# The first layer's recurrence gates as products of high and low parts, in a two-layer hybrid mixer on one core

## The chip, the core and the metric

The kernel runs on one core of a Trainium2 chip. The metric is the device time of one execution in microseconds (us), as a median over runs. TensorE (PE in the rows) multiplies, VectorE (DVE) and ScalarE (ACT) do elementwise work, GpSimd (POOL) fills tiles, and SyncE (SP) issues most of the transfers from memory.

## The reference

Two layers work on 256 context tokens and 256 latent tokens, 1024 wide, in float32. Each layer has a token mixer with three parallel branches behind one input projection (a long convolution, the RG-LRU recurrence, and HGRN2), their merge, and an MLP. Only the RG-LRU branch is touched. For each of its two directions it is

```python
xc = dwconv(xb, conv_w, conv_b, (LRU_CONV - 1, 0)).astype(F32)          # width 4
xh = xc.reshape(bsz, length, LRU_BLOCKS, LRU_BLOCK_DIM)                   # 8 blocks of 64
r = sigmoid(einsum('blhi,hij->blhj', xh, wr).reshape(bsz, length, E_LRU) + br)
i = sigmoid(einsum('blhi,hij->blhj', xh, wi).reshape(bsz, length, E_LRU) + bi)
log_a = -LRU_C * r * softplus(-lam)
a = exp(log_a)
b = sqrt(-expm1(2.0 * log_a)) * (i * xc)
h_t = a_t * h_{t-1} + b_t
```

The two `einsum`s are the gates: block-diagonal products of the convolved input `xc` (512 channels) with the matrices `wr` and `wi`.

## The kernel before, in words

Channels lie on the 128 partitions and tokens along the row, 256 of the context and 256 latent ones side by side, so that a tile is 128x512. The 512 channels of the RG-LRU are four such tiles, c = 0 to 3, each with two directions d. Two blocks of 64 stand on the diagonal of one 128x128 matrix, so a gate of one (d, c) is one product of 128x128 with 128x512. A layer has 16 of them: 4 tiles, 2 directions, 2 gates.

**Precision.** The large products of the kernel are made of three: an operand is written as a high part (a copy rounded to the type float32r, `cp` on ScalarE or a cast on VectorE) and a low part (the difference, `sub` on VectorE), and `three` (L689) accumulates high x high, high x low and low x high in one bank. A float32 product without parts is one call in the program, which the trace shows as two TensorE instructions, each with a weight load of its own.

**The gates.** `lru_gates` (L925) takes the column x of the projection, makes the convolution `xc` (one `affine` on ScalarE, three `stt` on VectorE), then the two gate products, their sigmoids, `xc * i`, and a tanh. In the second layer (`l == 1`) `xc` and the gate matrices are split into parts and go through `three`; in the first they are multiplied as float32.

**The gate matrices.** They are loaded at the beginning of `layer` (L1269). The first layer has four float32 tiles filled by transfers that ScalarE's queue issues (`dma2`). The second has one buffer of 128x2048 that SyncE's queue fills in four transfers (`dma`), and eight tiles of parts made from it.

**Buffers.** Nearly all 128x512 tiles (`blk`, tile name b) come from one pool of 49 slots; this holds the normalised input in parts (16 slots in the first layer), the projected columns, the states of the recurrence and the gate matrices. The weights come in pieces of 1 MB into `raw_tile`, of which there are two (tile name ra); these two also take the pieces of `w_ada` for the modulation that are multiplied in between (`ada_steps`, L372). A weight piece is split into four tiles wh and wl (`weight`, L635), whose pool has four of each; when the `wl` differences are made, the buffer is free for the next transfer.

**The order of the work.** A scheduler orders the instructions of each engine by priority and by its own model of the times; a few stretches are ordered by hand (`InOrder.fixed`), and the stretch around the first layer's gates isn't one of those. The first layer's mixer projects columns one group after the other (`columns`, L1294); after each it takes a step of the generator `recurrences` (L1358) and one of the background generator that holds `ada_steps`. So the gates of c = 0 and 1 stand among the columns of LRU_G and the products of w_i, with the first scans behind them, and those of c = 2 and 3 among the columns after that. The calls of all engines pass through one helper, so that the trace puts nearly everything on L220; tile names tell the groups apart: px<-b,b of 128x512 are the gate products, wh and wl the weights' parts, pm the projections.

Of the kernel before, what the change touches and what calls it, by code (L numbers as in the profile page):

```python
# [9 lines left out]
F32 = mybir.dt.float32  # L10
F32R = mybir.dt.float32r
# [151 lines left out]
def _body(ctx, tc, I, out, cfg):  # L163
# [12 lines left out]
    def nm(s):  # L176
        counter[0] += 1
        return f"{s}{counter[0]}"

    def blk(dt=F32, p=128, w=512, late=""):  # L180

        x = bp.tile([p, w], dt, tag="b", name=nm("b"), padded_shape=[128, 512])
        if late and late in cfg["LATE"]:
            nc.gpsimd.memset(x[:, 0:1].bitcast(F32) if dt is not F32 else x[:, 0:1], 0.0)
        return x
# [10 lines left out]
    def psm():  # L196
        return pm.tile([128, 512], F32, tag="m", name=nm("pm"))

    def psx(kind):
        for i, (kinds, n) in enumerate(cfg["PX"]):  # L200
            if kind in kinds:
                return px.tile([128, 512], F32, tag=f"x{i}", name=nm("px"), bufs=n)
# [37 lines left out]
    def fn(o, i, f, bias=0.0, scale=1.0, accum=None):  # L240

        ins = act.activation(o, i, f, bias=bias, scale=scale, accum_out=accum).ins
        tc.add_manual_dep(ins, tables[1].name, no_sync, reason="activation tables in order")
        tables[0].append(ins)
# [7 lines left out]
    def affine(o, i, scale, bias):  # L252
        return act.activation(o, i, AF.Identity, bias=bias, scale=scale).ins

    def cp(o, i):
        return act.activation(o, i, AF.Copy).ins

    def tt(o, a, b, op):
        dve.tensor_tensor(o, a, b, op=op)

    def mul(o, a, b):
        tt(o, a, b, ALU.mult)
# [4 lines left out]
    def sub(o, a, b):  # L267
        tt(o, a, b, ALU.subtract)

    def stt(o, a, s, b, op0=ALU.mult, op1=ALU.add):  # L270
        dve.scalar_tensor_tensor(o, a, s, b, op0=op0, op1=op1)
# [9 lines left out]
    def mm(p, l, r, start, stop, **k):  # L281
        last_mm[0] = pe.matmul(p, l, r, start=start, stop=stop, **k).ins
        return last_mm[0]
# [5 lines left out]
    def v3(a, n):  # L289
        return a.rearrange("p (a b) -> p a b", b=n)  # L290

    dma = nc.sync.dma_start
    dma2 = nc.scalar.dma_start
# [14 lines left out]
    def col(l, name, i, n=1):  # L308
        return vec[l][:, V[name] + i:V[name] + i + n]
# [27 lines left out]
    def raw_tile():  # L337
        return wp.tile([128, 2048], F32, tag="raw", name=nm("ra"), bufs=cfg["RAW"])
# [350 lines left out]
    def three(p, lh, ll, rh, rl, start, stop):  # L689
        mm(p, lh, rh, start, False)  # L690
        mm(p, lh, rl, False, False)
        return mm(p, ll, rh, False, stop)
# [232 lines left out]
    def lru_gates(l, d, c, x, bd, sp_pos):  # L925
        xc = blk()
        affine(xc, x, col(l, "cw", d * 16 + 12 + c), col(l, "cb", d * 4 + c))
        x3, o3 = v3(x, 256), v3(xc, 256)
        for s in (1, 2, 3):
            w = col(l, "cw", d * 16 + (3 - s) * 4 + c)  # L930
            if d == 0:
                stt(o3[:, :, s:], x3[:, :, :256 - s], w, o3[:, :, s:])
            else:
                stt(o3[:, :, :256 - s], x3[:, :, s:], w, o3[:, :, :256 - s])
        r, i = blk(late='r'), blk(late='r')
        if l == 1:
            hi, lo = blk(F32R), blk(F32R)
            cp(hi, xc)
            sub(lo, xc, hi.bitcast(F32))
        for g, o in ((0, r), (1, i)):  # L940
            p = psx('l')
            cs = slice(c * 128, c * 128 + 128)
            if l == 1:
                three(p, bd[d][g][0][:, cs], bd[d][g][1][:, cs], hi, lo, True, True)
            else:
                mm(p, bd[d][g][:, cs], xc, True, True)
            fn(o, p, AF.Sigmoid, bias=col(l, ("br", "bi")[g], d * 4 + c))
        mul(xc, xc, i)
        fn(i, r, AF.Tanh, scale=sp_pos[:, d * 4 + c:d * 4 + c + 1])
        return xc, r, i  # L950
# [22 lines left out]
    def lower_bounds(l):  # L973

        om, nom, lbf = kt([128, 4]), kt([128, 4]), kt([128, 4])
        if l == 0:
            pool.memset(om, 1.0)
            pool.memset(nom, -1.0)
            pool.memset(lbf, F_FLOOR)
            return om, nom, lbf  # L980
        m, e, s = small(), small(), small()
        v0, v1 = col(l, "lb", 0, 4), col(l, "lb", 4, 4)
        tt(m[:, :4], v0, v1, ALU.max)
        sub(e[:, :4], v0, m[:, :4])
        sub(e[:, 4:], v1, m[:, :4])
        fn(e, e, AF.Exp)
        add(s[:, :4], e[:, :4], e[:, 4:])
        dve.reciprocal(s[:, :4], s[:, :4])
        mul(e[:, :4], e[:, :4], s[:, :4])
        mul(e[:, 4:], e[:, 4:], s[:, :4])  # L990
        add(m[:, :4], e[:, :4], e[:, 4:])
        sub(m[:, :4], m[:, :4], e[:, :4])
        ts(om, m[:, :4], -1.0, 1.0)
        ts(nom, m[:, :4], -1.0, None, op0=ALU.add)
        ts(lbf, m[:, :4], F_FLOOR, None, op0=ALU.add)
        return om, nom, lbf
# [272 lines left out]
    def layer(l, S, xs=None, es=None):  # L1269
# [6 lines left out]
        lnexp()  # L1276
        sp_neg, sp_pos = softplus_neg(l)
        lbs = lower_bounds(l)
        if l == 1:
            raw, bd = raw_tile(), [[None, None], [None, None]]  # L1280
            for d in range(2):
                for g in range(2):
                    r = raw[:, (2 * d + g) * 512:(2 * d + g) * 512 + 512]
                    dma(r, I["bd"][l, d, g].rearrange("p c n -> p (c n)"))
                    bd[d][g] = blk(F32R), blk(F32R)
                    cp(bd[d][g][0], r)
                    sub(bd[d][g][1], r, bd[d][g][0].bitcast(F32))
        else:
            bd = [[blk() for _ in range(2)] for _ in range(2)]
            for d in range(2):  # L1290
                for g in range(2):
                    dma2(bd[d][g], I["bd"][l, d, g].rearrange("p c n -> p (c n)"))

        def columns(c0, n, lat, take, first=False):  # L1294

# [62 lines left out]
        def recurrences():  # L1358
            for half in range(2):
                cs = (2 * half, 2 * half + 1)  # L1360
                sigmoid()
                for c in cs:
                    for d in range(2):
                        lru_st[d, c] = lru_gates(l, d, c, xs[c], bd, sp_pos)
                        yield
                if half == 1:
                    while len(lg) < 4 // per:
                        yield
                    for x in lg:
                        gelu(x)  # L1370
                    if l in cfg["MG"]:
                        while not pairs:
                            yield
                        hg_sigmoids(*pairs[0])
                lnexp()
                for c in cs:
                    for d in range(2):
                        lru_decay(d, c, lru_st[d, c], sp_neg)
                        lru_h[d, c] = lru_scan(d, lru_st[d, c])
                    add(lru_h[0, c], lru_h[0, c], lru_h[1, c])  # L1380
                    yield
# [108 lines left out]
        for bi, b in enumerate(cfg["ORD"][l]):  # L1490
# [12 lines left out]
            for r in range(2):  # L1503
# [3 lines left out]
                for i in range(4 * r // per, 4 * (r + 1) // per):  # L1507
                    p = psm()
                    for j in range(per):
                        c = i * per + j - 4 * r  # L1510
# [302 lines left out]
    for _ in f0:  # L1813
        pass
    bg.put(ada_steps(0, 1))
    S1, es = layer(0, S0, xs)
    layer(1, S1, None, es)


# [14 lines left out]
```

## Time and profile before

| what | value |
|---|---|
| three runs | 1484.55, 1487.90, 1488.62 us; median 1487.9 us |
| the profiled execution | 1488.52 us, of which the span from the first to the last instruction is 1486.7 us |
| granted TensorE clock, mean | 0.995 of full speed |
| TensorE busy | 1456.6 us (98%) |
| VectorE busy | 1072.7 us (72%) |
| ScalarE busy | 745.4 us (50%) |

A matmul's row gives its start and its length with the pipeline's depth, so lengths of neighbours overlap; the spacing of their ends is what each costs. The idle time that a row shows in brackets is that of its engine just before it, with what ended it.

### The profile page before, as it was taken

Reading aid. Unit: us, or ns where it says so; the run is one execution under the profiler, and the core shown is the slowest. Engines: PE = TensorE matmul, PEld = TensorE weight load, DVE = VectorE, ACT = ScalarE, POOL = GpSimd, SP = SyncE. Lnnn points to the kernel's source line nnn. Section 1 sums busy time; section 2 is a strip of 40 time slices with the busy share of each in tenths; the row PEclk is TensorE's granted clock in tenths of the full one; section 3 lists DMA queues with packets and bytes.
Section 4 is the critical chain, followed back from the end, with each engine's and each line's share of the span. In section 5 each row is a group of like instructions: output and inputs, shape, how many; then the busy total and the mean of one; then the engine's idle time right before and its main releaser. Section 6 shows DMA issues by size and latency. Waiting matters only on the chain.

```text
span 1486.7 us, 21716 instructions
## 1 busy us (share of the span) xinstructions
PE 1456.6 (98%) x8326; PEld 1224.5 (82%) x8326; DVE 1072.7 (72%) x1853; ACT 745.4 (50%) x1188; POOL 25.2 (2%) x245
## 2 busy tenths in 40 slices
PE   8999999999999999999999999999999999999998
PEld 4766878888888888888887877798889999899986
DVE  6776397978996277755757985776799886866544
ACT  6476565642232425543331223568877745565433
POOL 1000000000000000000000000000000000000000
PEclk9999999999999999999999999999999999999999
DMA  9644321232562242545745534132325335445553
GB/s 316 233 182 160 127 86 58 73 112 86 177 242 91 99 140 88 176 157 189 269 147 208 201 130 141 58 143 85 114 88 178 147 138 204 156 171 186 198 196 113
DMA packets 56999, 225.38 MB, mean 152 GB/s; under 512 B 6448, under 2 KB 8112, under 8 KB 37312
## 3 DMA queue, kind: packets, MB, share of 16 engines
q1 hardware_dynamic: 55168, 220.86, 42.3%
q10 hardware_dynamic: 1728, 3.15, 0.6%
q8 instruction: 65, 1.06, 0.3%
q14 instruction: 38, 0.31, 0.1%
HBM read 220.80 MB, written 3.18 MB: 151 GB/s over the span
## 4 chain that ended last, share of the span: by engine, by line
PE 82%; DVE 9%; ACT 5%; issue 2%; DMA 1%; SPq 0%; DVEq 0%; POOL 0%; ACTq 0%; POOLq 0%
PE pm L220 73%; PE px L220 9%; DVE b L220 4%; DVE t L220 2%; DVE wl L220 2%; ACT b L220 2%; ACT t L220 2%; ACT wh L220 1%; DVE s L220 1%; ACT L220 1%; DMA h<-in_x_dram 1%; DMA k<-in_w_ada_dram 0%; DMA ra<-in_w_ada_dram 0%; DVE h L220 0%; ACT s L220 0%
## 5 line engine op out<-in xcount | busy, mean ns | idle before, releaser
L220 PE MATMUL pm<-b,wh 128*128 128x512 f32 (+1 forms) x3264 | 822.0, 342 | 1.7 <-DVE b L220 1.7
L220 PEld LDWEIGHTS pm<-b,wh 128*128 128x128 f32 x3264 | 564.0, 190 | 76.2 <-issue 3.5
L220 PE MATMUL pm<-b,wl 128*128 128x512 f32 (+1 forms) x1632 | 556.8, 341 | 0.0
L220 ACT ACTIVATE wh<-ra 128x1024 fp32r<-128x1024 f32 x278 | 293.5, 1060 | 498.2 <-PE pm L220 485.3
L220 DVE TENSOR_TENSOR wl<-ra,wh 128x1024 fp32r<-128x1024 f32 x278 | 338.4, 1222 | 243.1 <-ACT wh L220 235.3
L220 PEld LDWEIGHTS pm<-b,wl 128*128 128x128 f32 x1632 | 310.3, 190 | 34.7 <-issue 1.3
L220 PE MATMUL pm<-wh,b 128*128 128x512 f32 x976 | 304.3, 392 | 1.1 <-DVE b L220 1.1
L220 PEld LDWEIGHTS pm<-wh,b 128*128 128x128 f32 x976 | 182.4, 188 | 46.3 <-issue 3.6
L220 PE MATMUL pm<-wl,b 128*128 128x512 f32 x488 | 190.7, 391 | 0.0
L220 DVE TENSOR_TENSOR b<-b,b 128x512 fp32r<-128x512 f32 (+2 forms) x179 | 120.5, 681 | 30.4 <-PE pm L220 14.7
L220 DVE SCALAR_TENSOR_TENSOR t<-k,k,t 128x512 f32<-128x512 f32 x168 | 117.3, 747 | 15.6 <-DMA k<-in_w_ada_dram 15.6
L220 PEld LDWEIGHTS pm<-wl,b 128*128 128x128 f32 x488 | 91.6, 188 | 20.5 <-issue 1.6
L220 PE MATMUL pm<-b,b 128*128 128x256 f32 (+1 forms) x456 | 77.3, 324 | 2.3 <-DVE b L220 2.3
L220 ACT ACTIVATE t<-t 128x512 f32<-128x512 f32 (+3 forms) x124 | 60.8, 526 | 30.7 <-DVE t L220 29.6
L220 PEld LDWEIGHTS pm<-b,b 128*128 128x128 f32 x456 | 66.7, 190 | 10.1 <-DVE b L220 3.6
L220 ACT ACTIVATE t<-pm 128x512 f32<-128x512 f32 (+1 forms) x74 | 42.4, 574 | 35.8 <-PE pm L220 33.3
L220 ACT ACTIVATE b<-pm 128x512 f32<-128x512 f32 x88 | 50.5, 583 | 18.9 <-PE pm L220 10.9
L220 PE MATMUL px<-b,b 128*128 128x128 f32 (+1 forms) x280 | 55.3, 344 | 2.1 <-ACT b L220 1.3
L220 ACT ACTIVATE b<-b 128x512 f32<-128x512 f32 (+1 forms) x80 | 48.7, 627 | 10.7 <-DVE b L220 9.6
L220 ACT ACTIVATE b<-b,k 128x512 f32<-128x512 f32 x64 | 45.7, 739 | 8.6 <-DVE b L220 8.3
L220 PEld LDWEIGHTS px<-b,b 128*128 128x128 f32 x280 | 38.4, 190 | 12.6 <-issue 6.0
L220 ACT ACTIVATE t<-px 128x384 f32<-128x384 f32 (+3 forms) x50 | 21.9, 438 | 46.8 <-PE px L220 46.6
(114 smaller groups left out, 1060.3 us busy)
## 6 DMA issues: line engine op xcount, KB each, us to landing
ra<-in_w_mlp_dram SPq DMA_DIRECT2D x63, 1024.0 KB, 4.9
ra<-in_w_in_dram SPq DMA_DIRECT2D x58, 1024.0 KB, 4.9
k<-in_w_ada_dram SPq DMA_DIRECT2D x128, 256.0 KB, 3.8
ra<-in_w_proj_dram SPq DMA_DIRECT2D x12, 1024.0 KB, 4.8
b<-in_w_ada_first_dram SPq DMA_DIRECT2D x32, 256.0 KB, 5.3
ra<-in_w_ada_dram SPq DMA_DIRECT2D x8, 1024.0 KB, 5.8
ra<-in_w_out_dram SPq DMA_DIRECT2D x8, 1024.0 KB, 5.2
ra<-in_w_i_dram SPq DMA_DIRECT2D x4, 1024.0 KB, 4.7
```

The lines of the kernel that those rows point to most:

```text
L220: r = f(*a, **k)
```

## The change

The first layer's gates are written as the second layer's: `xc` is split into `hi` and `lo`, the gate matrices are loaded into one raw buffer by SyncE's queue and split into eight tiles, and each gate is a `three`.

```diff
         r, i = blk(late='r'), blk(late='r')
-        if l == 1:
-            hi, lo = blk(F32R), blk(F32R)
-            cp(hi, xc)
-            sub(lo, xc, hi.bitcast(F32))
+        hi, lo = blk(F32R), blk(F32R)
+        cp(hi, xc)
+        sub(lo, xc, hi.bitcast(F32))
         for g, o in ((0, r), (1, i)):
             p = psx('l')
             cs = slice(c * 128, c * 128 + 128)
-            if l == 1:
-                three(p, bd[d][g][0][:, cs], bd[d][g][1][:, cs], hi, lo, True, True)
-            else:
-                mm(p, bd[d][g][:, cs], xc, True, True)
+            three(p, bd[d][g][0][:, cs], bd[d][g][1][:, cs], hi, lo, True, True)
...
-        if l == 1:
-            raw, bd = raw_tile(), [[None, None], [None, None]]
-            for d in range(2):
-                for g in range(2):
-                    r = raw[:, (2 * d + g) * 512:(2 * d + g) * 512 + 512]
-                    dma(r, I["bd"][l, d, g].rearrange("p c n -> p (c n)"))
-                    bd[d][g] = blk(F32R), blk(F32R)
-                    cp(bd[d][g][0], r)
-                    sub(bd[d][g][1], r, bd[d][g][0].bitcast(F32))
-        else:
-            bd = [[blk() for _ in range(2)] for _ in range(2)]
-            for d in range(2):
-                for g in range(2):
-                    dma2(bd[d][g], I["bd"][l, d, g].rearrange("p c n -> p (c n)"))
+        raw, bd = raw_tile(), [[None, None], [None, None]]
+        for d in range(2):
+            for g in range(2):
+                r = raw[:, (2 * d + g) * 512:(2 * d + g) * 512 + 512]
+                dma(r, I["bd"][l, d, g].rearrange("p c n -> p (c n)"))
+                bd[d][g] = blk(F32R), blk(F32R)
+                cp(bd[d][g][0], r)
+                sub(bd[d][g][1], r, bd[d][g][0].bitcast(F32))
```

## Rows read from the trace of the kernel before

**Rows 1.** Busy time by stage: PE, PEld, DVE, ACT, POOL, clock, DMA share, GB/s.
```profile
90.00:105.00 15.00, 15.00 (x65) 9.26 (x65) 13.09 (x19) 13.28 (x20) 0.10 (x1) 1.00 0.67 256
105.00:120.00 15.00, 15.00 (x74) 10.53 (x73) 13.44 (x19) 14.40 (x22) 0.43 (x5) 1.00 0.48 174
120.00:135.00 15.00, 13.62 (x57) 8.94 (x56) 8.24 (x12) 8.18 (x12) 0.29 (x3) 1.00 0.58 203
150.00:175.00 25.00, 25.00 (x112) 20.69 (x111) 5.52 (x5) 8.71 (x12) 0.10 (x1) 1.00 0.38 144
```

**Rows 2.** The chain that ended last, 91 to 130 us: start, us, what.
```profile
91.86 1.73 PE px L220 x4
...
109.55 4.18 DVE b L220 x6
...
121.39 1.14 DVE wl L220
...
123.13 1.15 DVE wl L220
124.28 0.01 issue
124.29 4.94 DMA ra<-in_w_ada_dram
```

**Rows 3.** TensorE in order of time, first layer's gates and the wait after them.
```profile
74.36 1.88 PE L220 MATMUL px<-b,b 128*128 128x512 f32 x4
...
78.69 1.96 PE L220 MATMUL px<-b,b 128*128 128x512 f32 x4
...
119.99 0.39 PE L220 MATMUL pm<-wl,b 128*128 128x512 f32 x1
120.22 3.59 PE L220 MATMUL px<-b,b 128*128 128x512 f32 x8
123.25 1.03 PE L220 MATMUL pm<-b,wh 128*128 128x512 f32 x2
...
129.28 1.06 PE L220 MATMUL px<-ra,k 128*32 128x512 f32 x8 [1.38 <-DMA ra<-in_w_ada_dram]
...
136.96 1.96 PE L220 MATMUL px<-b,b 128*128 128x512 f32 x4
...
145.42 1.96 PE L220 MATMUL px<-b,b 128*128 128x512 f32 x4
```

**Rows 4.** TensorE in order of time, second layer's gates in three products.
```profile
1004.74 0.39 PE L220 MATMUL pm<-wl,b 128*128 128x512 f32 x1
1004.97 2.88 PE L220 MATMUL px<-b,b 128*128 128x512 f32 x12
1007.69 0.62 PE L220 MATMUL pm<-wh,b 128*128 128x512 f32 x2
...
1045.08 0.73 PE L220 MATMUL px<-b,b 128*128 128x512 f32 x2 [1.30 <-ACT b L220]
...
1046.85 1.20 PE L220 MATMUL px<-b,b 128*128 128x512 f32 x4 [0.57 <-DVE b L220]
```

**Rows 5.** Chain that ended last, a dense stretch of projections.
```profile
375.95 74.16 PE pm L220 x327
```

**Rows 6.** Groups by form: count, busy us, mean ns, idle before.
```profile
L220 PEld LDWEIGHTS pm<-b,wh 128*128 128x128 f32 x3264 | 564.0, 190 | 76.2 <-issue 3.5 <-ACT wh L220 3.4 <-DVE b L220 2.6
L220 DVE TENSOR_TENSOR b<-b,b 128x512 fp32r<-128x512 f32 x101 | 69.5, 688 | 19.4 <-PE pm L220 14.7 <-ACT b L220 3.0
L220 DVE TENSOR_TENSOR b<-ra,b 128x512 fp32r<-128x512 f32 x36 | 23.0, 684 | 12.1 <-ACT b L220 12.1
L220 ACT ACTIVATE b<-ra 128x512 fp32r<-128x512 f32 x36 | 20.2, 625 | 24.7 <-DMA ra<-in_w_out_dram 11.8 <-DMA ra<-in_w_mlp_dram 6.7 <-DMA ra<-in_w_in_dram 6.1
L220 ACT ACTIVATE b<-b 128x512 fp32r<-128x512 f32 x12 | 7.4, 625 | 9.6 <-DVE b L220 9.6
```

**Rows 7.** All engines in order of time, 62 to 74 us.
```profile
62.17 0.33 SPq L632 DMA_DIRECT2D ra<-in_w_in_dram  x1
62.88 0.85 ACTq L1292 DMA_DIRECT2D b<-in_bd_dram  x2
63.77 1.05 ACTq L1292 DMA_DIRECT2D b<-in_bd_dram  x2
...
68.02 2.35 DVE L220 TENSOR_TENSOR wl<-ra,wh 128x1024 fp32r<-128x1024 f32 x2
...
73.65 0.60 ACT L220 ACTIVATE b<-pm 128x512 f32<-128x512 f32 x1 [3.07 <-PE pm L220]
```

**Rows 8.** VectorE in order of time, its two pauses between 91 and 126 us.
```profile
103.88 1.29 DVE L220 SCALAR_TENSOR_TENSOR b<-t,b 128x512 f32<-128x512 f32 x2 [1.70 <-ACT t L220]
106.59 1.23 DVE L220 TENSOR_TENSOR wl<-ra,wh 128x1024 fp32r<-128x1024 f32 x1 [1.42 <-ACT wh L220]
```

**Rows 9.** GpSimd in order of time: the first write of the tiles r and i.
```profile
60.88 0.46 POOL L184 MEMSET b<- 128x1 f32 x12
...
110.81 0.13 POOL L184 MEMSET b<- 128x1 f32 x2 [5.42 <-DVE b L220]
```

## The prediction

> **What bounds the kernel now.** I began with the page: TensorE is busy for 98% of the span, so nearly every microsecond that its work loses or gains is seen at the end, unless a wait gives it back. The gates of the first layer lie between 74 and 148 us, so I read that stretch next, by stages [rows 1]. TensorE shows no idle time from 90 to 120 us, but VectorE is busy for 13.1 and 13.4 of each 15 us there and ScalarE for 13.3 and 14.4. So three engines are near full at once, and work can't be moved from one to another for nothing. From 150 to 175 us VectorE has 5.5 of 25 us: whatever it owes is paid off by then, and what the change does to the time is settled before 150 us.
>
> The third view is the chain that ended last [rows 2]. At 91.86 us it passes through the gate products and then runs on VectorE and ScalarE, not on TensorE: recurrence steps (the 4.18 us row is six of them) and the wl differences of the weights, up to 124.28 us. There the last wl difference frees one of the two raw buffers, a w_ada piece is sent for, and TensorE waits 1.38 us for it at 129.28 us [rows 2, 3]. This is the one wait of TensorE itself in the whole stretch. To the left of it TensorE is full, but what it finishes early there it would only wait longer for.
>
> **The products.** Four float32 gate products stand in the eight-instruction row at 120.22 us. The product before them ends at 119.99 + 0.39 = 120.38, the second one behind them at 123.25 + 1.03 = 124.28 [rows 3]. Of these 3.90 us two ordinary products take 2 x 0.227, by the dense stretch where 327 take 74.16 us [rows 5]. So one float32 gate product costs 3.45 / 4 = 0.86 us. The second layer shows what replaces it: twelve instructions are four gate products; the one before ends at 1005.13, the second one behind at 1008.31, and (3.18 - 0.454) / 4 = 0.68 us each [rows 4], which is three times 0.227. The gain is 0.18 us a product and 16 x 0.18 = 2.9 us of TensorE's time in all.
>
> **Where that gain counts.** The products of c = 0 (four, at 74.36 and 78.69 us [rows 3]) come before the VectorE chain; what they save, 4 x 0.18 = 0.7 us, moves the start of the chain, because its columns come from TensorE. The four products of c = 1 and the four of c = 2 stand beside the chain. TensorE would come to the w_ada product 8 x 0.18 = 1.4 us earlier and wait that much longer: they give nothing while VectorE sets the end. The four of c = 3, at 136.96 and 145.42 us [rows 3], come after it and save 0.7 us again. So 1.4 us of the 2.9 count, if that wait stays.
>
> **The splits of xc.** Each of eight (d, c) gets a copy on ScalarE, 0.625 us, and a difference on VectorE, 0.688 us, as the second layer's do [rows 6]. Those of c = 0 fall before 80 us and those of c = 3 after 130 us, where VectorE has room. Four of them fall beside the chain: 4 x 0.688 = 2.75 us on VectorE and 4 x 0.625 = 2.5 us on ScalarE. The lower bound is nothing: VectorE pauses 1.70 and 1.42 us between 91 and 126 us [rows 8], 3.1 us, which would hold them all. The upper bound is the full 2.75 us, because both pauses wait for ScalarE, which has 2.3 us free in 30 [rows 1] and is loaded as well. I take the middle, 1.4 us later at the w_ada piece.
>
> **The wait on hi and lo.** A product now also needs two more steps before it, 0.625 + 0.688 = 1.3 us. The order of TensorE's queue is fixed before the run, so a late part stops everything behind it. The second layer shows it: at the first gate of its second half TensorE waits 1.30 us for ScalarE's hi and then 0.57 us for VectorE's lo [rows 4], 1.9 us; at its other gates I find no such wait. The bounds are 0 and 2 x 1.9 us, one for each half. In the place where I expect it, at c = 1 or c = 2, it lies in front of the 1.38 us wait, and TensorE would wait there anyway, so I charge nothing for the forecast and keep 1.9 us for the range.
>
> **The gate matrices.** Removed are four transfers by ScalarE's queue, at 62.88 us, which occupy it for 0.85 + 1.05 = 1.9 us [rows 7]; added are four on SyncE's queue, which has only weights to issue there and issues one in 0.33 us [rows 7], four copies of 0.625 us on ScalarE (2.5 us, so 0.6 net) and four differences of 0.684 us on VectorE (2.7 us) [rows 6]. They come before 70 us, ahead of the chain. The one thing on a path is the raw buffer: the matrices hold one of the two until the last difference, and the second weight of LRU_G, sent for at 62.17 us [rows 7], and the first w_ada piece queue for what is left. If all of the four splits came in front of that transfer, it would be 4 x (0.625 + 0.684) = 5.2 us late. Its own split ends at 70.37 us and TensorE comes to it when the column before is done, about 73.65 us [rows 7]: 3.3 us of slack. The bounds are 0 and 5.2 - 3.3 = 1.9 us. The first weight's transfer is no longer queued behind a w_ada piece, so the slots shift by one place and the splits should find their gap near 60 us; I take 0.
>
> **The sum.** 1488.52 - 0.7 - 0.7 + 1.4 = 1488.5 us against the profiled execution's own time, so no change. That execution stands 0.6 us above the median of the three runs; moved to the median this is 1487.9, and I say 1488.0 us. A difference of 0.3%, 4.5 us, is about what a measurement of this kernel can tell from no change; all of the terms together are smaller.
>
> **The rivals.** *The whole gain comes through.* If the scheduler finds room for the splits, or puts the w_ada product later in TensorE's order, the 2.9 us count in full, and up to 1.38 us of the wait [rows 3] goes as well: 1487.9 - 2.9 = 1485.0, at best 1483.6. For it: 3.1 us of pauses on VectorE. Against it: both engines are near full where it matters [rows 1]. Chance 0.14.
>
> *All of the added work is on the path.* VectorE's 2.75 us in full, one stop of 1.9 us for hi and lo outside the cover, and the late buffer's 1.9 us, with 1.4 us back: 1487.9 + 5.1 = 1493.0 at the end, about 1491 if one of the three is covered. For it: each of the three has a row. Against it: they follow one another, and a stop early on gives VectorE time to catch up. Chance 0.18.
>
> *Slower by the pool of 49.* The change keeps eight gate tiles where four were, and two more for each gate in hand. GpSimd's first writes tell how full the pool is: twelve r and i tiles are taken at 60.88 us, and the next two only at 110.81 us, after a wait for VectorE's reads [rows 9]. So from 61 to 110 us the slots may be all in use, and with four to eight fewer an evacuation of a projection has to wait for a slot. TensorE then runs on until its four accumulation banks are full and stops. It decides from the point where an evacuation is later than the banks cover, a column or two of 8 x 3 products, 24 x 0.227 = 5.4 us each. The price is that of the gate which gives the slot back: three convolution steps on VectorE (0.7 us each, by its row for a difference), the two splits and the two products, 3 x 0.7 + 1.3 + 2 x 0.68 = 5 us, to twice that: 1493 to 1498. Against it: the tiles of c = 2 were taken some 40 us before their use, and taking them later costs nothing. Chance 0.14.
>
> *The three products are no cheaper.* Each of the three loads its own weights, 0.190 us a load [rows 6]. Were loads not hidden behind the product before, a gate would cost 3 x (0.227 + 0.190) = 1.25 us against 0.86, and the 16 would lose 16 x 0.39 = 6.2 us: 1494. The spacing of 0.227 us over 327 products that each load weights [rows 5] and the second layer's 0.68 [rows 4] speak plainly against it. Chance 0.02. The Trainium skill's TensorE: Matmul & The Clock Gate, in the section on packing small matmuls, states such a rule: weight loads overlap with running matmuls only when they use other rows of the array, which 128-row weights never do. By its figure for a load (128 columns at 1.2 GHz, 0.107 us) my estimate for a gate would be 1.0 us, a loss of 2.2 us in all where the rows give a gain of 2.9; the trace disagrees with the rule as it would apply here.
>
> **How the numbers follow.** The forecast, no net change within some 2 us either way and a scatter of the scheduler's order on top, has 0.52. Chances: gain in full 0.14, all on the path 0.18, pool 0.14, loads 0.02. Below 1483.4 us (0.3% under the median): a third of the full gain's cases, with a fresh order of the rest of the layer, and 0.04 of the forecast's, 0.09. Above 1492.4: the last two cases nearly whole, 0.15, a third of the second, 0.06, and 0.01 of the forecast's, 0.22. The rest, 0.69, is no change. For 8 in 10 I go from 1483.5 to 1495.0; the forecast's own range is 1485.5 to 1490.5.
>
> **What would show it.** In the changed profile the gates of the first layer should stand as twelve instructions for four products, 0.68 us each. The granted clock should stay at full speed. VectorE should have 8 x 0.688 more from 70 to 150 us. TensorE's wait for a w_ada piece near 128 us should be longer than 1.38 us, by what its products have saved and VectorE's splits cost. A wait of pm on ACT b or DVE b at a gate shows a late part; a wait of TensorE on an evacuation near 90 to 150 us, the pool. I am wrong if that w_ada wait is gone, or if a new wait of more than 3 us appears, or if later stretches, beyond 200 us, have been put in another order with gaps of another size.

## The result and the profile after

The change made the kernel slower: 1496.64 us median (1491.19 to 1498.42, 7 runs) against 1488.25 us (1484.55 to 1489.12, 7 runs), a ratio of 1.0056 with the interval 1.0042 to 1.0071. I had said 1488.0 us and no change; the time lies above the range as well. The profiled execution took 1496.64 us with a span of 1494.7 us.

Busy time by stage answers to [rows 1]; the columns are PE, PEld, DVE, ACT, POOL, granted clock, DMA share and GB/s.

```profile
105.00:120.00 15.00, 15.00 (x75) 10.94 (x73) 12.56 (x17) 13.95 (x22) 0.33 (x4) 1.00 0.59 237
120.00:135.00 15.00, 8.14 (x35) 4.02 (x28) 11.24 (x17) 9.81 (x17) 0.49 (x7) 0.77 0.51 170
135.00:150.00 15.00, 14.73 (x66) 11.56 (x64) 9.23 (x13) 8.68 (x14) 0.19 (x2) 1.00 0.27 94
```

One stage stands out: from 120 to 135 us TensorE has 8.14 us of work where it had 13.62, and the granted clock is 0.77. TensorE in order of time shows what happened; it answers to [rows 3].

```profile
118.47 0.39 PE L220 MATMUL pm<-wl,b 128*128 128x512 f32 x1
118.69 0.84 PE L220 MATMUL px<-b,b 128*128 128x512 f32 x3
119.47 1.06 PE L220 MATMUL px<-ra,k 128*32 128x512 f32 x8
120.46 0.96 PE L220 MATMUL px<-b,b 128*128 128x512 f32 x3
128.29 2.36 PE L220 MATMUL px<-b,b 128*128 128x512 f32 x4 [6.86 <-ACT b L220]
130.58 1.66 PE L220 MATMUL px<-ra,k 128*32 128x512 f32 x8
132.17 0.74 PE L220 MATMUL px<-b,b 128*128 128x512 f32 x2
132.75 0.63 PE L220 MATMUL pm<-b,wh 128*128 128x512 f32 x2
```

The last products of v end at 118.86 us. Behind them stand only the four gate products of c = 2 and one w_ada product. TensorE finishes the two of d = 0 (three instructions each), then waits 6.86 us for ScalarE's hi of d = 1. The wait for a w_ada piece [rows 3] is gone. The next w_ada product takes 1.66 us where the one before the stop took 1.06. The chain that ended last answers to [rows 2]:

```profile
120.85 2.33 DVE wl L220 x2
123.19 4.40 DVE b L220 x7
...
127.61 0.64 ACT b L220
...
128.29 4.63 PE px L220 x14
```

It no longer ends in a transfer but in the convolution for d = 1, c = 2 (three of the seven VectorE instructions in the second row), ScalarE's hi, and the gate. ScalarE in order of time, first after the change and then before it, shows who stood behind that hi:

```profile
121.15 0.80 ACT L220 ACTIVATE b<-b,k 128x512 f32<-128x512 f32 x1
...
127.61 0.63 ACT L220 ACTIVATE b<-b 128x512 fp32r<-128x512 f32 x1 [1.42 <-DVE b L220]
128.14 2.04 ACT L220 ACTIVATE b<-pm 128x512 f32<-128x512 f32 x4
```

```profile
111.03 0.60 ACT L220 ACTIVATE b<-pm 128x512 f32<-128x512 f32 x1
...
113.81 0.58 ACT L220 ACTIVATE b<-pm 128x512 f32<-128x512 f32 x1
...
116.76 0.58 ACT L220 ACTIVATE b<-pm 128x512 f32<-128x512 f32 x1
...
121.15 0.58 ACT L220 ACTIVATE b<-pm 128x512 f32<-128x512 f32 x1
```

The four copies b<-pm take v out of its four accumulation banks. Before, they came one by one, the last at 121.15 us. After, all four stand behind hi in ScalarE's queue and come at 128.14 us, and the convolution's first step (b<-b,k) starts at 121.15 us. The four follow one another without a gap, so by then all four had a place; since when, no row shows. GpSimd's first writes of r and i answer to [rows 9]:

```profile
61.30 0.29 POOL L184 MEMSET b<- 128x1 f32 x7
75.83 0.10 POOL L184 MEMSET b<- 128x1 f32 x1 [14.23 <-PE px L220]
85.87 0.10 POOL L184 MEMSET b<- 128x1 f32 x1 [9.94 <-PE px L220]
```

Seven tiles find a place at once where twelve did; the eighth and the ninth wait until TensorE's products for px have read a tile. As far as these writes show, the pool of 49 is full at 61 us and gives places only one by one after that.

### The profile page after: what moved, and what is told of

It reads as the page before. It is cut to its first block, busy times and chain, and to the rows that moved or that the text cites. A ratio compares the mean times of both kernels' runs of the same rounds, so it can differ in the third digit from the quotient of the medians.

```text
span 1494.7 us, 21779 instructions
## 1 busy us (share of the span) xinstructions
PE 1459.6 (98%) x8342; PEld 1230.0 (82%) x8342; DVE 1080.5 (72%) x1865; ACT 751.6 (50%) x1200; POOL 25.4 (2%) x245
## 3 DMA queue, kind: packets, MB, share of 16 engines
q8 instruction: 65, 1.06, 0.3%
## 4 chain that ended last, share of the span: by engine, by line
PE 80%; DVE 11%; ACT 6%; issue 2%; DMA 1%; DVEq 0%; SPq 0%; ACTq 0%; POOL 0%; POOLq 0%
PE pm L220 70%; PE px L220 10%; DVE b L220 5%; DVE t L220 3%; DVE wl L220 2%; ACT b L220 2%; ACT t L220 2%; ACT wh L220 1%; DVE s L220 1%; DMA k<-in_w_ada_dram 1%; ACT L220 1%; ACT s L220 0%; DMA ra<-in_w_ada_dram 0%; DVE h L220 0%; DMA h<-in_ctx_dram 0%
## 5 line engine op out<-in xcount | busy, mean ns | idle before, releaser
L220 DVE TENSOR_TENSOR b<-b,b 128x512 fp32r<-128x512 f32 (+2 forms) x187 | 125.9, 683 | 33.1 <-ACT b L220 16.1
L220 ACT ACTIVATE b<-b 128x512 f32<-128x512 f32 (+1 forms) x88 | 53.7, 627 | 22.5 <-DVE b L220 20.6
L220 PEld LDWEIGHTS px<-b,b 128*128 128x128 f32 x296 | 41.4, 194 | 21.4 <-ACT b L220 10.9
```

What stands on the lines that cost most here:

```text
L220: r = f(*a, **k)
```

## The experiments

Three theories stood against each other at the start. P: the stop comes from hi and lo taking places in the pool of 49. W: the splits' own work makes hi late. O: the order of claims matters, not the number of places. Later V joined: it is v's copies that find no place, and the late gate is only what TensorE runs into. All ratios are against the kernel before.

**hi and lo in temporary tiles.**

```diff
-        hi, lo = blk(F32R), blk(F32R)
+        hi, lo = (tmp(F32R), tmp(F32R)) if l == 0 else (blk(F32R), blk(F32R))
```

> The change with one edit: hi and lo of the first layer's xc are taken from the pool of 14 temporary tiles, not from the pool of 49. All work stays. Theory P (slots): the 6.86 us stop of TensorE at the gate of d = 1, c = 2 comes from that pool; with hi and lo out of it the second convolution of c = 2 is made early again, the stop is gone, and the time comes back to 1485 to 1489 us. Rival W (work): ScalarE's copies and VectorE's differences themselves make hi late; nothing of them is removed, so a stop of 5 to 8 us stays and the time is 1494 to 1498 us.

Measured: 1485.53 us median of 11, ratio 0.9988 (0.9976 to 0.9999). All work is there, and the stop before the gates of d = 1, c = 2 is gone. What is left of TensorE's waits from 100 to 150 us is 1.1 us before the last of the four gate products, and it is not for hi, which is a tile t in this version, but for a sigmoid of ScalarE:

```profile
PE px L220 <- ACT b L220: 1.1, 1, 1.1
```

W falls: 11.1 us against the change come back with no work removed.

**The low gate matrices in temporary tiles too.**

```diff
-                bd[d][g] = blk(F32R), blk(F32R)
+                bd[d][g] = blk(F32R), blk(F32R) if l == 1 else tmp(F32R)
```

> The change with hi and lo and also the four low gate matrices of the first layer from the pool of temporary tiles: the claims on the pool of 49 are then those of the kernel before. Theory P: no stop, 1485 to 1489 us, and within 1 us of the kernel that moves hi and lo alone if the four resident tiles do no harm, 1 to 3 us below it if they do. Rival W: a stop of 5 to 8 us, 1494 to 1498 us.

Measured: 1484.67 us median of 12, ratio 0.9985 (0.9975 to 0.9995), 0.9 us below the version before it, which is less than either of them scatters (1483.51 to 1486.63 us there, 1481.95 to 1488.22 us here). Its gates show the price of the products, with v's last copy at 119.17 us:

```profile
118.24 0.62 PE L220 MATMUL px<-t,b 128*128 128x512 f32 x2
118.70 0.39 PE L220 MATMUL px<-t,t 128*128 128x512 f32 x1
118.93 0.62 PE L220 MATMUL px<-t,b 128*128 128x512 f32 x2
119.39 0.39 PE L220 MATMUL px<-t,t 128*128 128x512 f32 x1
119.61 0.62 PE L220 MATMUL px<-t,b 128*128 128x512 f32 x2
...
120.38 0.72 PE L220 MATMUL px<-t,b 128*128 128x512 f32 x2
...
121.18 0.62 PE L220 MATMUL pm<-b,wh 128*128 128x512 f32 x2
...
126.53 1.07 PE L220 MATMUL px<-ra,k 128*32 128x512 f32 x8 [0.40 <-DMA ra<-in_w_ada_dram]
```

Four gate products lie 0.69, 0.68, 0.77 and 0.80 us apart. The w_ada product comes 2.75 us earlier than before [rows 3], and its wait has not grown but shrunk to 0.40 us. Of the 2.75 us, 1.2 us stand already at the second w_i piece, which is sent for at 89.59 us against 90.77.

**The low gate matrices alone.** The last edit by itself, hi and lo back in the large pool.

> The change with the four low gate matrices in temporary tiles, hi and lo of xc in the large pool. If the four resident tiles fill the pool, the stop at d = 1, c = 2 is gone and the time is 1485 to 1490 us; if the two tiles that each gate takes for hi and lo do it, the stop of 6 to 7 us stays and the time is 1494 to 1498 us.

Measured: 1492.19 us median of 9, ratio 1.0035 (1.0021 to 1.0048). The stop is there in full, 6.77 us, with v's four copies behind hi again:

```profile
124.98 0.63 ACT L220 ACTIVATE b<-b 128x512 fp32r<-128x512 f32 x1 [1.42 <-DVE b L220]
125.52 2.04 ACT L220 ACTIVATE b<-pm 128x512 f32<-128x512 f32 x4
```

So the stop does not need the four resident tiles. The time lies between the two spans given for it, so neither held as written. From the transfer of the second w_i piece to that of the first w_proj piece the profile takes 253.2 us, as the change's does (253.5); the 4.5 us less in the median are not from this stretch. Of the 4.7 us between the two profiles 2.8 us lie before the second w_i piece (90.20 us against 92.97), where the clock granted from 10 to 20 us was 0.83 here and 0.66 in the change; the rest I have not followed.

**Three places more in the large pool.**

```diff
-CFG = dict(NB=49, NT=14, RAW=2, WB=4,
+CFG = dict(NB=52, NT=12, RAW=2, WB=4,
```

> The change with three slots more in the large pool (52 for 49) and two fewer temporary tiles (12 for 14). Theory P in its simplest form, too few slots: three more than half make up for the four gate tiles that are kept longer, the stop falls under 3 us and the time is 1486 to 1491 us. Variant O of it, that the order in which tiles take their turn in the pool puts the late convolution behind, whatever the count within a few slots: the same stop of 6 to 7 us, 1494 to 1498 us. Rival W: also 1494 to 1498 us.

Measured: 1498.52 us median of 5, ratio 1.0079 (1.0065 to 1.0093); the stop is unchanged:

```profile
123.83 2.37 PE L220 MATMUL px<-b,b 128*128 128x512 f32 x4 [6.84 <-ACT b L220]
```

Three places don't cure it. GpSimd takes eight r and i tiles at once there instead of seven, so one of the three seems to have gone to a later gate's tile.

**The claims on the pool alone.** The kernel before, with four tiles held and two more in each gate.

```diff
+        held = [blk(late='r') for _ in range(4)] if l == 0 else []
...
+            pair = blk(), blk()
+            for x in pair:
+                act.activation(x[:, 0:1], xc[:, 0:1], AF.Copy)
...
```

> The kernel before, float32 products and no splits, with the change's claims on the pool of 49 alone: four tiles more held from the start of the layer to the last gate, and two more in each gate, each written in one column. Theory P: the pool alone delays a convolution or an evacuation near 105 to 130 us, a stop of TensorE of 3 to 7 us stands there and the time is 1491 to 1497 us. Rival W: no splits, so no stop beyond the 1.4 us for the w_ada piece, 1487 to 1490 us.

Measured: 1488.31 us median of 12, ratio 1.0006 (0.9993 to 1.0018), the longest stop at a gate 1.31 us. The simple form of P falls here: as many claims by themselves bring no stop, and by the interval they cost between -1.0 and 2.7 us. v's copies come in pairs at 121.35 and 123.25 us, not behind the gate.

**The splits alone.** The kernel before with its float32 products, and hi and lo written to temporary tiles and read by nobody.

> The kernel before with its float32 products, plus the copies and differences of xc in the first layer (into temporary tiles, read by nobody). It parts the price of the splits from the gain of the products. By the prediction's terms the splits cost 0 to 2.75 us, 1.4 us taken: 1488 to 1491 us. If they are hidden, as theory P has it, 1487 to 1488.5 us, which is the version with hi and lo in temporary tiles plus 2.9 us for the products. Rival W: they make a gate wait 3 us or more and the time is 1491 us or above.

Measured: 1487.64 us median of 11, ratio 0.9998 (0.9985 to 1.001). By the interval the splits cost between -2.2 and 1.5 us, and TensorE's one wait from 100 to 150 us is 0.8 us for the w_ada piece: as far as these runs can tell, they are hidden.

**Places of their own for v's four tiles.**

```diff
...
+    vkeep = [kt([128, 512]) for _ in range(4)]
...
-            x = blk()
+            x = vkeep[t]
             with tc.high_priority(200):
                 cp(x, pv[t])
```

> The change, with hi and lo left in the large pool, but the four tiles that take v's projections are given four places of their own (large pool 48, temporary tiles 12). Theory V: TensorE stops because v's projections fill all four accumulation banks and their copies out find no place in the pool, so that nothing but the late gate stands in its queue; with places of their own the copies come before 115 us, the stop falls under 2 us and the time is 1485 to 1489 us. Rival H: the late convolution of d = 1, c = 2 alone makes the stop, whatever v does; a stop of 4 to 7 us stays and the time is 1492 to 1498 us.

> The change with places of their own for the four v tiles, as before, but with all 14 temporary tiles (large pool 46), since 12 of them cost some 3 us in the second layer. Theory V: no stop over 2 us at d = 1, c = 2, and without that cost 1485 to 1488.5 us. Rival: the 4 to 5 us that the other version with places for v still lacked against hi and lo in temporary tiles come from the late convolution; then 1489 to 1492 us again.

Measured: 1490.22 us (median of 11, ratio 1.0013, 1.0001 to 1.0025) with 12 temporary tiles (the large pool then has 48 places) and 1490.02 us (median of 12, 1.0016, 1.0005 to 1.0026) with 14 (46 places). The second one's TensorE and ScalarE, in order of time:

```profile
119.95 0.96 PE L220 MATMUL px<-b,b 128*128 128x512 f32 x3
120.75 0.62 PE L220 MATMUL pm<-b,wh 128*128 128x512 f32 x2
...
127.57 0.39 PE L220 MATMUL pm<-b,wh 128*128 128x512 f32 x1
128.80 0.73 PE L220 MATMUL px<-b,b 128*128 128x512 f32 x2 [0.84 <-ACT b L220]
```

```profile
109.00 0.60 ACT L220 ACTIVATE k<-pm 128x512 f32<-128x512 f32 x1 [0.23 <-PE pm L220]
...
119.80 0.58 ACT L220 ACTIVATE k<-pm 128x512 f32<-128x512 f32 x1
...
128.12 0.63 ACT L220 ACTIVATE b<-b 128x512 fp32r<-128x512 f32 x1
```

This is the clearest picture of the case. The gate of d = 1, c = 2 is as late as in the change: hi comes at 128.12 us. But v's copies (k<-pm) come from 109.00 to 119.80 us, the banks are free, and TensorE works on the next projections in the meantime; the stop is 0.84 us. H falls, and V stands for the stop; one place more in all (46 and 4 against 49) can't be the reason, since three more alone changed nothing. For the time V does not stand: both medians lie above what it gave, by 1.2 and 1.5 us, and the second lies in the span of its rival (1489 to 1492 us), which blamed the late convolution for what is still missing. The stretch with that convolution is not where it is: from the second w_i piece to the first w_proj piece the version with 14 temporary tiles takes 246.1 us, the one with hi and lo in temporary tiles 246.3, the change 253.5. From there to the second layer's w_i pieces it needs 640.9 us against 639.0, in the second layer up to w_proj 188.5 against 187.8. The largest part of the 5.2 us between these two profiles, 2.7 us, lies before the second w_i piece (92.45 us against 89.78), ahead of any copy of v; there the clock granted from 10 to 20 us was 0.66 against 0.83. A single execution can't tell how much of that is in the medians, which lie 4.5 us apart, so that part stays open; the 12 temporary tiles were not the reason.

**All of the change but the three products.**

```diff
-            three(p, bd[d][g][0][:, cs], bd[d][g][1][:, cs], hi, lo, True, True)
+            if l == 1:
+                three(p, bd[d][g][0][:, cs], bd[d][g][1][:, cs], hi, lo, True, True)
+            else:
+                for y in (hi, lo):
+                    mm(p[:, :32], bd[d][g][1][:, cs], y[:, :32], True, True)
+                mm(p, bd[d][g][0][:, cs].bitcast(F32), xc, True, True)
```

> Everything of the change but the three products in the first layer: split gate matrices, hi and lo in the large pool and read by two products of 32 columns, whose result is overwritten, and one float32 product per gate with the high part of the matrix (its low part is left out). Theory J: the claims on the pool make the late order only together with the shorter products; no stop over 2 us, 1487.5 to 1490.5 us. Rival: claims and splits are enough, a stop of 5 to 7 us stands at d = 1, c = 2 and the time is 1494 to 1499 us.

Measured: 1491.82 us median of 6, ratio 1.0034 (1.0021 to 1.0048), 1.3 us above the span for J. But there is no stop; the waits of TensorE from 100 to 150 us are one:

```profile
PE px L220 <- DMA ra<-in_w_ada_dram: 0.2, 1, 0.2
```

The time above J's span agrees with the price of the added products. Three gates, with two small and two float32 instructions each, stand in one row (it is named by its first shape):

```profile
121.12 0.39 PE L220 MATMUL pm<-wl,b 128*128 128x512 f32 x1
121.35 3.41 PE L220 MATMUL px<-b,b 128*128 128x32 f32 x12
124.19 1.03 PE L220 MATMUL pm<-b,wh 128*128 128x512 f32 x2
```

From 121.51 to 125.22 us, less two products of 0.227, that is 1.08 us a gate against 0.86 [rows 3], and 16 x 0.22 = 3.5 us in all; the median lies 3.5 us above the kernel before.

So with longer gate products the late order does not come about, although hi, lo and v are all in the pool.

**The stop filled.** TensorE's queue gets 28, then 14 idle products in front of the late gate.

```diff
+            if (l, d, c, g) == (0, 1, 2, 0):
+                for _ in range(28):
+                    mm(p, bd[d][g][0][:, cs], bd[1 - d][g][0], True, True)
```

> The change, with 28 further products of gate matrices (28 x 0.227 = 6.4 us), whose result is overwritten, put in front of the first gate product of d = 1, c = 2, where TensorE stops for 6.86 us. Theory K: of the loss against the kernel before some 5 us are the clock, 3.3 us from 120 to 150 us (granted 0.89) and 1.8 us from 210 to 240 us (granted 0.94); with the gap filled the granted clock stays at 1.00 from 120 to 150 us and the time is 1491 to 1494 us. Rival: the gap itself is all of it, the clock comes back without a cost at the end, 1496 to 1498 us.

> The change with 14 further products (3.2 us) in TensorE's stop instead of 28, so that some 3.6 us of it stay empty. If any stop of that length makes the clock fall, it costs as much as with the stop empty: granted about 0.89 from 120 to 150 us, 1495 to 1497 us. If the length decides, the clock stays at full speed there in most runs and the time is 1490.5 to 1492.5 us, like the filled one.

Measured: 1491.07 us (median of 11, ratio 1.0027, 1.0015 to 1.0038) with 28 and 1494.6 us (median of 6, 1.0041, 1.0027 to 1.0055) with 14, where 3.67 us of the stop stay. The windows from 120 to 150 us of TensorE, for the change, for 28 and for 14 products (busy, clock, DMA share, GB/s):

```profile
120.00:150.00 30.00, 22.87 (x99) 0.89 0.39 132
```

```profile
120.00:150.00 30.00, 28.84 (x130) 1.00 0.38 139
```

```profile
120.00:150.00 30.00, 26.06 (x110) 0.94 0.38 141
```

Six microseconds of work for nothing make the kernel 5.6 us faster by the medians, 4.4 us by the means. The profiles place 3.3 us of it here (30 us at 0.89 instead of 1.00); the rest I could not place, and near 210 us the clock fell in the filled version's profile too. The change's own seven executions agree that the clock, and not only the stop, sets the time: five with a mean granted clock of 0.988 to 0.990 took 1496.54 to 1498.42 us, while one with 0.993 took 1491.19 and one with 0.996 took 1492.48 us. A stop of 3.67 us still lets the clock fall, though not always: with 14 products five executions have 0.991 or 0.992 and 1494.01 to 1495.74 us, and one has 0.998 and 1489.44 us. For 14 products the median lies between the two spans, so neither form of the expectation held as written.

**The second layer's hi and lo in temporary tiles as well.**

```diff
-        hi, lo = blk(F32R), blk(F32R)
+        hi, lo = tmp(F32R), tmp(F32R)
```

> The version with hi, lo and the low gate matrices in temporary tiles, and hi and lo of the second layer there too. If the second layer's wait of 1.9 us at its first gate of the second half comes from the large pool as well, it goes and the time is 1482 to 1484 us; if it is the two steps of the split themselves, 1484 to 1486 us, no change.

Measured: 1486.95 us median of 12, ratio 1.0 (0.999 to 1.0011). Nothing is gained in the second layer, and the median lies above the span of 1484 to 1486 us. At the same gate TensorE still waits 1.15 us for hi and 0.34 us for lo, where it waited 1.29 and 0.57 us in the version with both edits: the pool is not what makes it wait there.

## Why the prediction was wrong

**The products: the price was right, what counts was not.** Three products take 0.68 to 0.80 us for a forecast of 0.68. I let only 1.4 of the 2.9 us count, because TensorE would wait longer for the w_ada piece. Where the stop is cured, more than that comes through: 1487.64 - 1484.67 = 3.0 us between the version with the splits alone and the one with both edits (1.9 us by their ratios), and there the w_ada wait shrank to 0.40 us. The chain on VectorE was not a wall: its last wl difference ended at 124.28 us [rows 2], and in that version it ends at 121.34 us.

**The splits: 0 to 2.75 us, 1.4 us taken.** Measured between -2.2 and 1.5 us: the lower bound lies inside, the value taken at the edge, the upper bound outside.

**The wait on hi and lo: this is the step that failed.** I wrote: "it lies in front of the 1.38 us wait, and TensorE would wait there anyway, so I charge nothing for the forecast and keep 1.9 us for the range." The wait came at c = 2, where I expected it. It took 6.86 us, not 1.9, and the 1.38 us that should have covered it was gone. The upper bound came from the second layer [rows 4], where TensorE comes to the gate at 1043.78 us and the convolution ends 0.6 us later. Here TensorE came at 121.43 us and the convolution ended at 127.58, 6.15 us later, and TensorE's queue held nothing else in front of the gate. The last convolution step, in the second layer before the change and then here:

```profile
1043.62 0.74 DVE L220 SCALAR_TENSOR_TENSOR b<-b,k,b 128x506 f32<-128x506 f32 x1
```

```profile
126.83 0.75 DVE L220 SCALAR_TENSOR_TENSOR b<-b,k,b 128x506 f32<-128x506 f32 x1
```

A bound for a wait has to ask what the engine could do meanwhile; in the version with places for v the same late gate costs 0.84 us.

**The gate matrices: 0 to 1.9 us, 0 taken.** The amount was right: TensorE's one wait between 60 and 75 us in the changed profile, 0.31 us, is for the first hi and not for them. The reason given was not: all four splits came in front of the weight's transfer, which is sent for at 68.67 us, when the last difference ends, and not at 62.17 us. TensorE had other products until then.

**The clock: "should stay at full speed".** It did not: 0.77 from 120 to 135 us. The version with 28 filling products lies 5.6 us below the change, and 5.5 us above the version with hi and lo in temporary tiles: so by the medians, of the 11.1 us between the change and that version about half is the stop and half the clock, of which the profiles place 3.3 us behind the stop. That version lies 2.3 us below the kernel before (1485.53 against 1487.86); 11.1 - 2.3 = 8.8 us, where 8.4 us were measured. The Trainium skill's TensorE: Matmul & The Clock Gate, in the section HAM oscillation — how this bites in real kernels, warns of this: a gap in TensorE's work is paid twice, once as idle time and once as work at the lower clock. The runs agree in kind, with 5.5 and 5.6 us by the medians.

**The rivals.** *Slower by the pool of 49* is what happened, at a chance of 0.14 and a price of 1493 to 1498 us: an evacuation of a projection finds no place, TensorE runs until its four banks are full and stops. Its mechanism is shown from both ends, by hi and lo taken out of the pool and by v taken out. Two of its parts were wrong. I had the price as a gate's 5 to 10 us with no word of the clock, so that the time lies in that span is partly luck. And the number of places is not what decides: three more don't help, and as many claims without the shorter products bring no stop. The order that the scheduler writes into ScalarE's queue tips, and the runs show three things that each tip it back (hi and lo elsewhere, v elsewhere, longer products). Why it tips with the three together was not settled, nor whether the copies of v lacked a place at run time or only in the scheduler's own model. *The whole gain* at 1485.0 us is what the change does once hi and lo are elsewhere: 1485.5 and 1484.7 us. *All on the path* and *loads not hidden* played no part.

**The signs I named.** Three instructions a gate at 0.68 us: yes, 0.67 us for the gate at 118.69 us. A clock at full speed: no. 8 x 0.688 = 5.5 us more on VectorE from 70 to 150 us: 4.0 us (59.66 against 55.65). A wait of more than 3 us and the w_ada wait gone: both stood in the text as signs of being wrong, and both came.

## What to carry to other kernels

Before tiles are added to a shared pool, list what else takes its place there in the same stretch, and above all the copies that empty accumulation banks: a bank that can't be emptied stops TensorE, however small the new tiles' own work. Short-lived parts such as hi and lo belong in a pool of short-lived tiles; here that one line is worth 11.1 us and turns a loss of 0.56% into a gain of 0.12%, with an interval that almost reaches no change. And where the clock falls behind a stop of TensorE, the stop costs about twice: here by the medians 5.5 us of idle time and 5.6 us that came back with the clock.

## What the runs showed of the hardware

The same wait of 3.1 us on TensorE stands in every profile, with its end between 202.6 and 212.9 us, and what the clock does behind it differs from one to the next. In the kernel before, where the wait ends at 207.02 us, it stays at full speed; in the version with all hi and lo in temporary tiles, where it ends at 203.89 us, it is granted 0.51, about the lower of its two levels (1.2 GHz), from 205 to 210 us (busy, clock, DMA share, GB/s; the kernel before first):

```profile
205.00:210.00 5.00, 2.98 (x47) 1.00 0.35 146
210.00:215.00 5.00, 5.00 (x26) 1.00 0.00 0
```

```profile
205.00:210.00 5.00, 5.00 (x50) 0.51 0.02 3
210.00:215.00 5.00, 5.00 (x24) 1.00 0.00 0
```

The clock goes with most of what scatters from run to run. Over 83 runs of the kernel before, the time follows the mean granted clock with a correlation of -0.88: at 0.997 the median is 1484.9 us (12 runs), at 0.992 it is 1490.6 us (10 runs). A difference of a few microseconds between two single runs of this kernel says nothing until their clocks are compared.
